# Layer 0 of a hybrid RWKV-7 / attention trunk: a pair's nine value products in one run behind its outputs, and the sample chunk's outputs as one full-array product

## The chip, the cores and the metric

The kernel runs on one core of a Trainium2 chip. A core has five engines with instruction queues of their own: TensorE (PE; its weight loads are listed as PEld), VectorE (DVE), ScalarE (ACT), GpSimd (POOL) and SyncE (SP), which issues the DMA transfers here. They meet through semaphores. The metric is the device time of one execution in microseconds (us); the time of a version is the median of its runs.

## The reference

The reference is one inference step of a two-layer encoder trunk on 512 prompt tokens and 32 sample tokens, with 1024 channels, in fp32. Layer 0 mixes tokens by an RWKV-7 recurrence, layer 1 by differential attention; both add a four-head memory attention, a SiLU gate, an output projection and a residual. What matters here is the recurrence of layer 0, which each of 24 heads with 64 channels runs over the tokens:

```python
def step(S, inp):
    r_t, k_t, v_t, w_t, kk_t, a_t = inp
    sa = jnp.einsum('bhvk,bhk->bhv', S, -kk_t)
    S = (S * w_t[:, :, None, :] + sa[..., None] * (kk_t * a_t)[:, :, None, :]
         + v_t[..., None] * k_t[:, :, None, :])
    return S, jnp.einsum('bhvk,bhk->bhv', S, r_t)
```

S is a 64x64 state. The prompt starts from a zero state, the sample from a given one. Each head returns its outputs y and the last state.

## The kernel before

**Chunks and pairs.** The recurrence is computed in chunks of 64 tokens: chunks 0 to 7 are the prompt, chunk 8 is the sample. Two heads together fill 128 partitions and are one of 12 pairs. Within a chunk the step becomes small matrices: `at` (`ats` for the sample) holds, per chunk, the decayed scores and the inverse of a triangular system; `sv` (`svs`) holds the values in one half of the partitions and, once solved, the corrections in the other half; `bt` (`bts`) holds decayed keys; `zr` decayed queries. The chain of a chunk (`chunk`, L806) has three parts, each after a `yield`:

- a: `zr` times the state, then a VectorE addition into `avz` (not for chunk 0);
- b: the inverse times `avz` (the solve), two ScalarE copies of the result into `sv`, and, except for chunk 0, the ScalarE copy `yt` of a's other half and the scaled state `sd`;
- c: `bt` times `sv`, from which VectorE forms the next state in `SB` (prompt) or `SS` (sample).

`ps_c` are the PSUM tiles of the chain (pool `psc`, two buffers). `avz` is one tile for all chunks and pairs; it must hold, before a chunk's solve, the product of the chunk's scores with its values. These are the value products of `rw_values` (L782): for each chunk and each head of the pair one product with 64 rows and 64 columns, a quarter of the 128x128 array. An even chunk uses rows 0 to 63 and output columns 64 to 127, an odd one the other two halves. ScalarE copies them from PSUM (`ps_v`, pool `psm`, two buffers) into `avz`. The outputs (`rw_outputs`, L865; `outputs`, L799) are products of 128 rows and 64 columns, half of the array, into `ps_yc` (pool `psx`, one buffer), which VectorE adds to `yt`.

A product in fp32 is two instructions with a weight load each in the trace; the main products below use operands split in advance into a high and a low part, one instruction each.

**The order of work.** While layer 0 runs, `ordered` is set, and each engine's instructions are tied into the order in which the program issues them (`Queue`, `tie`): every queue is strictly in that order. The program writes it by a plan. The projections of the layer ("main products", PSUM tiles `ps_g`, 128x272 outputs, 48 to a block of weights) are a generator from which single products are drawn. `PLAN` (L49) has 23 steps for a pair; each step issues the next part of the chain (step 0 is b of chunk 0, step 1 its c, steps 2, 3, 4 are a, b, c of chunk 1, and steps 20, 21, 22 are a, b, c of chunk 7), and then two halves with listed pieces: `(kind, pair offset, TensorE cost, VectorE cost)`. The pieces are `prep` (the preparation of a later pair, some thirty small parts), `inv`, `back`, `at`, `mrg` (the triangular inverse on GpSimd, its transfers, its merge on TensorE), `val` (values), `out` (outputs), `fin` (norm and gate), `smp` (the sample chunk). After the pieces of each half, `some` may issue one or two put-off functions (weight splits, evacuation work on ScalarE and VectorE), and then main products are drawn while the counted time t is below the half's due time:

```python
while left and t + MAIN / 2 < (due[k + 1] if half else (due[k] + due[k + 1]) / 2):
    next(main)
    t += MAIN
    left -= 1
```

t adds up the plan's costs, 0.27 for a chain part (`HOP`) and 0.126 for a main product (`MAIN`). The due times divide the sum of all of a pair's costs into 23 equal steps where a pair has 144 main products or more; most pairs have 192.

**Around the change.** Before, the values come in two pieces. Step 21 of the pair before does chunks 0 and 8 (`("val", 1, 0.45, 0)`), step 0 of the pair itself chunks 1 to 7 (`("val", 0, 0.95, 0)`). Step 22 has the pair's outputs, and in its second half the part of the third-next pair's `prep` that computes two exponentials on ScalarE (`de`, and `di` in the place of `cum`). Step 0 has a transpose of that prep (`ps_rt`). Pair 0's values are made in a lead-in of four pieces ahead of the loop, as far as the first value piece goes. From pair 9 on there is no third-next pair, and memory attention takes the place of the prep.

The sample chunk is run by `smp` pieces; its outputs are two half-array products into the fourth quarter of its own `ps_c` tile (`self.outputs(st, (c,), ps, 3)`), added to `yt` by one VectorE instruction.

## Time and profile before

| | |
|---|---|
| median of 3 runs | 1459.28 us (1458.47 to 1459.82) |
| span of the profiled execution | 1461.1 us, its only time on record, 1.8 us over the median |
| TensorE busy | 1403.8 us, 96% of the span |
| VectorE, ScalarE, GpSimd busy | 915.4, 831.6, 421.5 us |
| mean granted TensorE clock | 0.986 |
| a middle pair of layer 0 | 45.9 us (for example from 330.6 to 376.5) |
| `ps_v<-sv,at`, prompt values | 384 records on TensorE |
| `ps_v<-svs,ats`, sample values | 48 records |
| `ps_yc<-sv,at`, prompt outputs | 384 records |
| `ps_c<-svs,ats`, sample outputs | 48 records |
| `avz<-ps_v`, value copies on ScalarE | 36: 12 each of 64x256, 64x384 and 64x512 |

A row of a timeline gives the start, the busy time, the engine, the line, the operation, the tiles (out<-in), for TensorE the part of the array that is used (rows*columns), the shape and how many instructions were merged into it; in brackets, how long the engine stood idle before it and what released it. L103 is the helper through which nearly every instruction goes, so tiles tell them apart. Tile names leave out buffer numbers; `cum` is also the place of `di`. The busy time of a TensorE row is modelled and overlaps with the next; the distance from start to start is what a row costs. The chain runs on a small set of tile names: `ps_c<-avz,at` is b, `ps_c<-sv,bt` is c, `ps_c<-SB,zr` is a.

### The profile page before, as it was taken

The page shows a single profiled execution, that of the slowest core. Times are in us where ns is not written, and L with a number is a line of the kernel's source. Part 1 is how long each engine was busy: PE and PEld are TensorE (multiplying, and loading weights), DVE is VectorE, ACT ScalarE, POOL GpSimd, SP SyncE. Part 2 cuts the span into 40 slices and gives each one's busy share as a digit, 9 for nine tenths or more (in the row PEclk, how much of TensorE's full clock was granted, in tenths as well). Part 3 has the DMA queues.
Part 4 walks back from the last instruction along what each step waited for, and adds up shares of the span by engine and source line. Part 5 has one row for each costly group of instructions (what it writes and reads, how often), then busy time and mean ns, then how long its engine had stood idle before and what let it go on. Part 6 is the DMA issues. An engine that isn't in the chain of part 4 may idle for free.

```text
span 1461.1 us, 32131 instructions
## 1 busy us (share of the span) xinstructions
PE 1403.8 (96%) x11978; PEld 1320.5 (90%) x11978; DVE 915.4 (63%) x2313; ACT 831.6 (57%) x2269; POOL 421.5 (29%) x868
## 2 busy tenths in 40 slices
PE   6998899999999999899899999999999999999997
PEld 5997899999999998798799998999989999899997
DVE  7565777787877877565733565664466745657533
ACT  6664667667677676565533365653466546565322
POOL 2025576566766557500210040100001002100200
PEclk9998999999999999999999999999999999999999
DMA  6442122332223222232554473232323222322321
GB/s 217 128 129 71 32 71 76 81 81 70 79 74 81 73 77 63 70 98 76 185 158 121 126 198 102 78 87 84 113 67 89 84 87 81 88 83 75 102 87 69
DMA packets 266534, 139.20 MB, mean 95 GB/s; under 512 B 57658, under 2 KB 256579, under 8 KB 266379
## 3 DMA queue, kind: packets, MB, share of 16 engines
q1 hardware_dynamic: 266378, 137.16, 33.1%
q8 instruction: 94, 1.54, 0.4%
q14 instruction: 62, 0.50, 0.1%
HBM read 110.98 MB, written 22.78 MB: 92 GB/s over the span
## 4 chain that ended last, share of the span: by engine, by line
PE 81%; DVE 8%; ACT 4%; issue 2%; DMA 2%; POOL 2%; SPq 1%; DVEq 0%; ACTq 0%; POOLq 0%
PE ps_g L103 56%; PE ps_c L103 4%; PE ps_s L103 3%; PE ps_o L103 2%; PE ps_at L103 2%; DVE wlo L103 1%; PE ps_v L103 1%; PE ps_mm L103 1%; SPq L103 1%; PE ps_mo L103 1%; POOL tm L721 1%; PE ps_ss L103 1%; PE ps_aT L103 1%; DVE pt L103 1%; PE ps_yc L103 1%
## 5 line engine op out<-in xcount | busy, mean ns | idle before, releaser
L103 PE MATMUL ps_g<-hh,wlo 128*128 128x272 f32 x1808 | 541.3, 299 | 1.4 <-DVE wlo L103 1.4
L103 PE MATMUL ps_g<-hh,whi 128*128 128x272 f32 x1808 | 540.1, 299 | 0.1
L103 PE MATMUL ps_g<-hl,whi 128*128 128x272 f32 x1808 | 535.6, 296 | 0.0
L103 DVE TENSOR_TENSOR wlo<-raw,whi 128x512 fp32r<-128x512 f32 x322 | 230.9, 728 | 205.6 <-ACT whi L103 196.2
L103 PEld LDWEIGHTS ps_g<-hh,wlo 128*128 128x128 f32 x1808 | 343.6, 190 | 6.4 <-DVE wlo L103 2.1
L103 PEld LDWEIGHTS ps_g<-hh,whi 128*128 128x128 f32 x1808 | 344.1, 190 | 4.4 <-PE ps_g L103 0.3
L103 PEld LDWEIGHTS ps_g<-hl,whi 128*128 128x128 f32 x1808 | 343.7, 190 | 3.6
L103 ACT CAST whi<-raw 128x512 fp32r<-128x512 f32 x322 | 194.7, 617 | 186.1 <-PE ps_g L103 132.6
L721 POOL TENSOR_TENSOR tm<-u,m 102x84 f32<-102x84 f32 (+23 forms) x372 | 158.3, 426 | 183.5 <-DMA m<-sc 155.4
L723 POOL TENSOR_TENSOR u<-u,tm 102x84 f32<-102x84 f32 (+23 forms) x372 | 158.5, 426 | 29.1
L103 PE MATMUL ps_g<-hi,whi 128*128 128x272 f32 x512 | 149.8, 292 | 0.9 <-ACT hi L103 0.9
L103 PE MATMUL ps_g<-lo,whi 128*128 128x272 f32 x512 | 148.4, 290 | 1.8 <-DVE lo L103 1.3
L103 PE MATMUL ps_g<-hi,wlo 128*128 128x272 f32 x512 | 148.3, 290 | 0.8 <-DVE wlo L103 0.8
L1706 POOL TENSOR_TENSOR kz<-k,kh 64x544 fp32r<-64x544 f32 x24 | 34.7, 1446 | 325.0 <-ACT kh L103 324.1
L103 PEld LDWEIGHTS ps_g<-lo,whi 128*128 128x128 f32 x512 | 96.9, 189 | 2.7 <-DVE lo L103 1.8
L103 PEld LDWEIGHTS ps_g<-hi,whi 128*128 128x128 f32 x512 | 97.0, 190 | 1.6 <-ACT hi L103 1.1
L103 PEld LDWEIGHTS ps_g<-hi,wlo 128*128 128x128 f32 x512 | 96.9, 189 | 1.1 <-DVE wlo L103 1.1
L103 DVE SCALAR_TENSOR_TENSOR SB<-ps_c,dl,sd 64x64 f32<-64x64 f32 x168 | 47.4, 282 | 49.0 <-PE ps_c L103 43.4
L103 ACT ACTIVATE pt<-ps_s,snm 128x128 f32<-128x128 f32 (+3 forms) x96 | 50.8, 530 | 23.8 <-DVE snm L103 23.0
L103 ACT COPY sv<-ps_c 64x64 f32<-64x64 f32 x192 | 39.5, 206 | 39.5 <-PE ps_c L103 37.7
L103 ACT ACTIVATE sg<-ps_g 128x272 f32<-128x272 f32 x64 | 25.3, 396 | 48.0 <-PE ps_g L103 45.5
L1161 POOL TENSOR_TENSOR lo<-og,hi 128x544 fp32r<-128x544 f32 x8 | 13.7, 1713 | 131.0 <-issue 130.5
(364 smaller groups left out, 2614.1 us busy)
## 6 DMA issues: line engine op xcount, KB each, us to landing
raw<-in_rw_in_dram SPq DMA_DIRECT2D x114, 256.0 KB
raw<-in_df_in_dram SPq DMA_DIRECT2D x112, 256.0 KB
raw<-in_w_out_dram SPq DMA_DIRECT2D x64, 256.0 KB
m<-sc SPq DMA_DIRECT2D x36, 128.0 KB
oscr<-sg SPq DMA_DIRECT2D x16, 272.0 KB
lo<-oscr SPq DMA_DIRECT2D x16, 272.0 KB
raw<-in_w_mem_k_dram SPq DMA_DIRECT2D x16, 256.0 KB
raw<-in_w_mem_v_dram SPq DMA_DIRECT2D x16, 256.0 KB
```

Of the source, the lines that this page charges most:

```text
L103: return lambda *a, **k: self.trunk.tie(self, issue(*a, **k))
L721: nc.gpsimd.tensor_tensor(tm[:, :n, :wd], u3[:, :n, kx : kx + 1].to_broadcast(sh), m3[:, kx : kx + 1, kx + 1 :].to_broadcast(sh), ALU.mult)
L723: nc.gpsimd.tensor_tensor(u3[:, :n, kx + 1 :], u3[:, :n, kx + 1 :], tm[:, :n, :wd], ALU.add)
L1161: (self.nc.gpsimd if g % 2 else self.ve).tensor_tensor(lo[:], t, hi[:].bitcast(F32), ALU.subtract)
L1706: nc.gpsimd.tensor_tensor(kz[rows[m], m, :], k[rows[m], :], hi.bitcast(F32), ALU.subtract)
```

## The change

The values of a pair become one piece, at step 22 of the pair before, behind the outputs and ahead of the exponentials: nine chunks, 18 products in one run, odd and even chunks in turn (1 with 0, 3 with 8, 5 with 2, 7 with 4, then 6 alone), into three PSUM tiles, one of them from the chain's pool `psc` and two from `psm`. Three ScalarE copies follow: chunks 0 and 8, then 2, 4, 6, then 1, 3, 5, 7. In the plan the pieces at step 0 (0.95) and step 21 (0.45) go, and one of cost 1.0 comes. In the lead-in all nine chunks of pair 0 are made where the first piece was.

The sample chunk's outputs become one product of the full array, 128 rows, 128 columns; only its two diagonal blocks are used. They lie in different partitions, so VectorE adds them to `yt` by two instructions in place of one.

```diff
-    [[("val", 0, 0.95, 0), ("prep", 2, 0.1, 0)], [("prep", 2, 0, 0.42)]],
+    [[("prep", 2, 0.1, 0)], [("prep", 2, 0, 0.42)]],
...
-    [[("prep", 3, 0, 1.45), ("val", 1, 0.45, 0)], [("prep", 3, 0, 0.5)]],
-    [[("out", 0, 1.6, 0.7)], [("prep", 3, 0, 0)]]]
+    [[("prep", 3, 0, 1.45)], [("prep", 3, 0, 0.5)]],
+    [[("out", 0, 1.6, 0.7), ("val", 1, 1.0, 0)], [("prep", 3, 0, 0)]]]
...
-        for sets in (((0, 8),), ((1, 3, 5, 7), (2, 4, 6))):
-            yield
-            ps = [self.psm.tile([P, 4, P], F32, tag="m", name=f"ps_v{cs[0]}") for cs in sets]
-            for j in range(len(sets[0])):
-                for h in range(2):
-                    for q, cs in zip(ps, sets):
-                        if j < len(cs):
-                            _, zs, ro, A, cv, _ = self.place(st, cs[j])
-                            self.te.matmul(q[zs, j, H[h]], A[0][ro, h, :], cv[ro, H[h]], start=True, stop=True)
-            for q, cs in zip(ps, sets):
-                e, zs = self.place(st, cs[0])[:2]
-                i = slice(0, 5, 4) if cs[0] == 0 else slice(cs[0] // 2, 4)
-                self.ae.copy(avz[zs, e, i, :], q[zs, : len(cs)])
+        yield
+        ps = [pool.tile([P, 4, P], F32, tag=tag, name=f"ps_v{i}")
+              for i, (pool, tag) in enumerate(((self.psc, "c"), (self.psm, "m"), (self.psm, "m")))]
+        sets = ((0, 8), (2, 4, 6), (1, 3, 5, 7))
+        for odd, even in zip((1, 3, 5, 7, None), (0, 8, 2, 4, 6)):
+            for h in range(2):
+                for c in (odd, even):
+                    if c is not None:
+                        q, cs = next((q, cs) for q, cs in zip(ps, sets) if c in cs)
+                        _, zs, ro, A, cv, _ = self.place(st, c)
+                        self.te.matmul(q[zs, cs.index(c), H[h]], A[0][ro, h, :], cv[ro, H[h]], start=True, stop=True)
+        for q, cs in zip(ps, sets):
+            e, zs = self.place(st, cs[0])[:2]
+            i = slice(0, 5, 4) if cs[0] == 0 else slice(cs[0] // 2, 4)
+            self.ae.copy(avz[zs, e, i, :], q[zs, : len(cs)])
...
         if c == 8:
-            self.outputs(st, (c,), ps, 3)
+            self.te.matmul(ps[:, 3, :], A[1].rearrange("p h t -> p (h t)"), cv, start=True, stop=True)
...
         if c == 8:
-            self.ve.tensor_tensor(yt[:64, 4, :], ps[:64, 3, :], yt[:64, 4, :], ALU.add)
+            for hc in H:
+                self.ve.tensor_tensor(yt[:64, 4, hc], ps[hc, 3, hc], yt[:64, 4, hc], ALU.add)
```

## The prediction

> **What bounds the kernel now.** I read the page first, then TensorE's waits, then the timelines of TensorE and ScalarE around one change of pairs, since the change works only there and at the sample chunk.
>
> ```profile
> span 1461.1 us, 32131 instructions
> PE 1403.8 (96%) x11978; PEld 1320.5 (90%) x11978; DVE 915.4 (63%) x2313; ACT 831.6 (57%) x2269; POOL 421.5 (29%) x868
> ```
>
> TensorE is busy 96% of the span. ScalarE's 57% looks harmless, but it is a mean over the program. The stretch from 281 to 289 us, where pair 2 ends and pair 3 begins, says something else:
>
> ```profile
> 281.00:289.00 8.00, 8.00 (x108) 7.44 (x108) 3.90 (x11) 7.30 (x21) 6.75 (x17) 1.00 0.37 107
> ```
>
> The columns after the length are the busy us of TensorE, its weight loads, VectorE, ScalarE and GpSimd, then the granted clock. TensorE is full, at full clock, and ScalarE has 0.70 us free in 8. What moves TensorE's work here must be asked of ScalarE too. TensorE's starts there:
>
> ```profile
> 281.10 0.38 PE L103 MATMUL ps_c<-avz,at 128*128 128x128 f32 x2
> 281.42 0.44 PE L103 MATMUL ps_v<-sv,at 64*64 64x64 f32 x4
> 281.70 0.39 PE L103 MATMUL ps_v<-svs,ats 64*64 64x64 f32 x4
> 282.02 0.39 PE L103 MATMUL ps_g<-hh,whi 128*128 128x272 f32 x1
> 282.25 0.29 PE L103 MATMUL ps_g<-hl,whi 128*128 128x272 f32 x1
> ...
> 283.12 0.38 PE L103 MATMUL ps_c<-sv,bt 128*128 128x128 f32 x2
> 283.44 1.15 PE L103 MATMUL ps_yc<-sv,at 128*64 128x64 f32 x32
> 284.52 0.40 PE L103 MATMUL ps_g<-hh,wlo 128*128 128x272 f32 x1
> 284.75 0.39 PE L103 MATMUL ps_c<-avz,at 128*128 128x128 f32 x2
> 285.07 1.14 PE L103 MATMUL ps_v<-sv,at 64*64 64x64 f32 x28
> 286.14 0.33 PE L103 MATMUL ps_rt<-ident,rr 128*128 128x128 f32 x1
> 286.22 0.37 PE L103 MATMUL ps_g<-hh,whi 128*128 128x272 f32 x1
> ...
> 286.92 0.38 PE L103 MATMUL ps_c<-sv,bt 128*128 128x128 f32 x2
> ...
> 288.90 0.38 PE L103 MATMUL ps_c<-SB,zr 128*128 128x128 f32 x2
> ```
>
> The ps_c rows are the chain: chunk 7's solve (281.10) and state product (283.12), chunk 0's solve (284.75) and state product (286.92), chunk 1's first product (288.90). I call them b7, c7, b0, c0, a1; b7 to a1 takes 7.80 us with 28 main products (ps_g) between: 8, 1, 5 and 14. A count is of records; one product of full precision is two. ScalarE, in its program order:
>
> ```profile
> 281.51 0.47 ACT L103 ACTIVATE ta<-ps_wa,dv 128x272 f32<-128x272 f32 x1
> 281.89 0.41 ACT L103 COPY sv<-ps_c 64x64 f32<-64x64 f32 x2
> 282.31 0.26 ACT L103 COPY yt<-ps_c 64x128 f32<-64x128 f32 x1
> 282.59 0.40 ACT L103 ACTIVATE sd<-SB,dl 128x128 f32<-128x128 f32 x1
> 283.02 0.37 ACT L103 COPY avz<-ps_v 64x256 f32<-64x256 f32 x1
> 283.41 0.67 ACT L103 ACTIVATE de<-cum 128x553 f32<-128x553 f32 x1
> 284.11 0.67 ACT L103 ACTIVATE cum<-cum 128x553 f32<-128x553 f32 x1
> 284.95 0.39 ACT L103 COPY raw<-ps_g 128x272 f32<-128x272 f32 x1 [0.17 <-PE ps_g L103]
> 285.23 0.30 ACT L103 COPY yt<-avz 64x128 f32<-64x128 f32 x1
> 285.54 0.42 ACT L103 COPY sv<-ps_c 64x64 f32<-64x64 f32 x2
> 286.24 1.08 ACT L103 COPY avz<-ps_v 64x512 f32<-64x512 f32 x2 [0.28 <-PE ps_v L103]
> ```
>
> Two orders matter. The two big value copies (1.08) come behind chunk 0's sv copies (end 285.96); and the exponentials of the prep (de, cum) run at 283.41, before chunk 0's solve. What a state product waits for is shown one pair earlier:
>
> ```profile
> 189.36 0.26 ACT L103 COPY yt<-ps_c 64x128 f32<-64x128 f32 x1
> ```
>
> ```profile
> 189.67 0.30 PEld L103 LDWEIGHTS ps_c<-sv,bt 128*128 128x128 f32 x2 [0.18 <-ACT yt L103]
> 190.09 1.01 PEld L103 LDWEIGHTS ps_yc<-sv,at 128*64 128x64 f32 x32
> ```
>
> ```profile
> 193.89 0.30 PEld L103 LDWEIGHTS ps_c<-sv,bt 128*128 128x128 f32 x2 [0.49 <-ACT sv L103]
> ```
>
> It starts 0.05 us after the end of the yt copy (189.62). Chunk 0 has no such copy; its state product was last released by sv (193.89). A c product that has waited takes 0.42 to the next start (189.67 to 190.09), one that has not 0.32 (283.12 to 283.44). Seven main products from 282.25 to 283.12 make 0.124 each; c0 to a1, 1.98, less 14 of these leaves 0.24 for two full records, 0.12 each.
>
> **The change, part by part.** *The plan.* Taking 0.95 from step 0 and 0.45 from step 21 and adding 1.0 to step 22 lowers a middle pair's sum by 0.40, so a step falls from 1.964 to 1.947 plan-us. Step 0 now counts 0.37 instead of 1.32 ahead of its main products: 13 in place of 5. Step 1 gets 13 for 14. Step 22 counts 0.27 + 1.6 + 1.0 = 2.87, more than a step, so it gets none for 1, and step 21 gets 4 for 8. b7 to a1 now holds 4 + 0 + 13 + 13 = 30.
>
> *b7 to c7.* Eight value records (281.42 to 282.02) and four main products leave. TensorE would be ready at 281.10 + 0.24 + 4 x 0.124 = 281.84. But c7 waits for the yt copy, whose work and predecessors are unchanged: 282.57 + 0.05 = 282.62. So 1.52 us for 2.02: -0.50, with 0.78 us of new idle. What is late is ScalarE's queue: ta, sv, sv, yt.
>
> *c7 to b0.* c7 takes 0.42, now that it waits; the outputs with their exit 1.08 (283.44 to 284.52). Of the 28-record run (1.07), the exit and four records in one quarter are known from the short visit (281.42, 281.70, 282.02: four records 0.28, four with the exit 0.32, so some 0.06 a record and 0.14 the exit); that leaves 0.03 for each of the 24 alternating ones, and eight more make 1.31. The switch from half to quarter arrays is not in the trace: free would be 0.12 less; I take the exit price, as a change of mode, and keep 0.12 below for the range. Sum 2.81 for 1.63: +1.18. In this segment one main product (0.23) leaves.
>
> *b0 to c0.* This decides. In program order ScalarE now has the three value copies, then the exponentials, then yt and sv of chunk 0. The copy of chunks 0 and 8 is early: chunk 8 stands in the second of four groups, so it runs beside the rest of the run and b0 does not wait. The others need the run's end; today the first starts 0.10 after it (286.14 to 286.24). From b0: 0.10 + 1.08 copies + 0.03 + 1.37 exponentials (283.41 to 284.78) + 0.02 + 0.30 yt + 0.01 + 0.42 sv + 0.05 = 3.38 us. TensorE meanwhile has b0 0.24, ps_rt 0.08 (286.14 to 286.22) and 13 x 0.124 = 1.61: 1.93 us. It idles 1.45; segment 3.38 for 2.17: +1.21. Nothing fills the hole, since c0 stands at the head of TensorE's queue and all main products of step 1 behind it. The raw, shc and rkv work of the finished block moves ahead of the value copies, into ScalarE's wait for them: free, or 0.39 more if the block's evacuation (284.95) were late.
>
> *c0 to a1.* One main product less, 0.10 for the restart: -0.02.
>
> The sum is -0.50 + 1.18 + 1.21 - 0.02 = +1.87; two main products more than before, 0.25, are missing elsewhere in the pair: **+1.62 us** per change of pairs. The same with no waits at all: b7 to c7 0.74, then 2.71, 1.93 and 1.86, less 0.25, is 6.99 for 7.80: -0.81. That is what the new order saves in array time.
>
> *Which boundaries.* There are eleven. In the first nine the prep of a third pair puts its exponentials there: 9 x 1.62 = 14.6. In the last two there are none; without their 1.37 the wait at c0 vanishes, but both ps_m buffers are held by value copies when the next products want them. I take +0.6 each (between -0.81 and +1.62): 1.2. Pair 0's own values move into the lead-in; TensorE's waits name the merge's transposes later in pair 0, and that wait covers the move either way.
>
> *Sample chunk.*
>
> ```profile
> 305.01 0.39 PE L103 MATMUL ps_c<-svs,bts 128*128 128x128 f32 x2
> 305.32 0.45 PE L103 MATMUL ps_c<-svs,ats 128*64 128x64 f32 x4
> 305.70 0.39 PE L103 MATMUL ps_g<-hh,wlo 128*128 128x272 f32 x1
> 305.93 0.29 PE L103 MATMUL ps_g<-hh,whi 128*128 128x272 f32 x1
> ```
>
> ```profile
> 305.96 0.58 DVE L103 SCALAR_TENSOR_TENSOR SS<-ps_c,dl,sd 64x64 f32<-64x64 f32 x2
> ```
>
> Four half-array records with their entry and exit become two full ones: 305.01 + 4 x 0.12 + 0.124 puts the second ps_g at 305.61 in place of 305.93, -0.32 (-0.2 if the entry were not the price that it looks). VectorE gets one more 64x64 addition; by half of a pair of them (305.96) about 0.29. It delays the sums queued behind it; the next chunk's solve hides that, and if its cover were gone it would cost 0.3. Eleven pairs count, as pair 0's gain goes into the wait above: -3.5.
>
> Total: 14.6 + 1.2 - 3.5 = +12.3 us. The profiled span of 1461.1 becomes 1473.4; the page gives no longer time of that execution, and the span stands 1.8 above the median of the runs, so I predict 1459.3 + 12.3 = **1471.6**.
>
> [...]
>
> **The rivals.** *The array time decides (faster).* If c7 and c0 find their operands ready, each boundary gains 0.81 and the sample chunk 0.32: 11 x 1.13 = 12.4, so 1446.9. For it: the entries and exits around 281.42, 283.44 and 285.07, of which one pair is left. Against it: ScalarE's 7.30 of 8. It decides if ScalarE has chunk 0's sv within 1.93 us of b0 instead of 3.38, as it would with the exponentials ahead of the value copies, and yt before 281.84.
>
> *Only c0 waits.* If c7's wait is covered (ScalarE reaches sv and yt earlier), 0.78 at each of eleven boundaries goes: 12.3 - 8.6 = +3.7, 1463.0. The 0.47 us of ta in front of sv speaks against it.
>
> *The edits cancel.* If only c7 waits, nine times 1.45 goes: 12.3 - 13.0 = -0.7, 1458.6, no change. It needs main products between b0 and c0 that the plan does not have, or shorter exponentials.
>
> *The waits spread.* If the held ps_m buffers and the late copies also hold up the next pair's prep, by 0.6 a boundary: +6.6, 1478.2.
>
> **How the numbers follow.** My sum 0.69, only c0 waits 0.09, array time 0.13, cancel 0.04, spread 0.05. The sum's own range is 1467 to 1476: down 1.3 for a free switch and 2.8 for the last two boundaries at -0.81, up 1.3 for the smaller sample gain and 2.0 for the last two at +1.62, and about 1 for the first boundary, whose work around it differs. A measurement of this kernel tells about 0.2%, 2.9 us, from no change. So faster 0.13, same 0.05, slower 0.82. The range 1462 to 1478 holds the main case, the one wait and part of the spread, about 0.8.
>
> **What would show it.** Right: c0 after each of nine boundaries starts 0.05 after ScalarE's sv, with an idle of about 1.4 before it; ScalarE's order there is three avz, de, cum, yt, sv; c7 waits about 0.8 for yt; ps_v and ps_yc stand in one unbroken run; the sample rows show x2 full products. Wrong: no idle before c0, or the exponentials ahead of the avz copies; then the array time wins and the forecast is off by over 20 us. If the c7 wait alone is missing, I misjudged what stands ahead of yt.

## The result, and the profile after

The changed kernel takes 1476.8 us (median of four executions; 1473.95 to 1495.83), the kernel before, run beside it, 1459.6. The ratio on record is 1.0148, 95% interval 1.0116 to 1.0180. It goes by all executions, and the one of 1495.83 lifts it; the medians alone make 1.0118. The forecast was 1471.6. The direction was right; of the loss of 17 us between the medians the forecast had 12. By the ratio the loss is some 22 us, which makes about 1481, and that lies above the range of the prediction.

The two counts at the head of the page of the changed kernel's profiled execution:

```profile
span 1472.2 us, 32129 instructions
PE 1392.4 (95%) x11954; PEld 1311.6 (89%) x11954; DVE 919.8 (62%) x2325; ACT 831.8 (56%) x2269; POOL 411.4 (28%) x868
```

TensorE is busy 11.4 us less than before, in a span that is 11.1 us longer: about 22 us of idle came in. Up to 6 of the 11.4 us can be the clock, since this execution was at half clock for 30.6 us and that of before for 42.7; the rest is saved array time. The same change of pairs as in the prediction, one pair later, by windows (length; busy us of TensorE, weight loads, VectorE, ScalarE, GpSimd; granted clock):

```profile
333.40:341.40 8.00, 6.49 (x98) 5.80 (x98) 3.24 (x12) 7.11 (x20) 6.66 (x18) 1.00 0.46 128
```

TensorE was busy all 8 us before; now it is busy 6.49, and ScalarE still 7.11. TensorE's starts there (timeline):

```profile
332.74 0.39 PE L103 MATMUL ps_c<-avz,at 128*128 128x128 f32 x2
...
334.25 0.49 PE L103 MATMUL ps_c<-sv,bt 128*128 128x128 f32 x2 [0.63 <-ACT yt L103]
334.67 1.15 PE L103 MATMUL ps_yc<-sv,at 128*64 128x64 f32 x32
335.75 0.50 PE L103 MATMUL ps_v<-sv,at 64*64 64x64 f32 x9
...
336.27 0.87 PE L103 MATMUL ps_v<-sv,at 64*64 64x64 f32 x20
337.07 0.49 PE L103 MATMUL ps_c<-avz,at 128*128 128x128 f32 x2
337.39 0.27 PE L103 MATMUL ps_rt<-ident,rr 128*128 128x128 f32 x1
...
340.18 0.49 PE L103 MATMUL ps_c<-sv,bt 128*128 128x128 f32 x2 [0.88 <-ACT sv L103]
...
342.14 0.27 PE L103 MATMUL ps_c<-SB,zr 128*128 128x128 f32 x1
```

Both waits of the forecast are there: c7 on yt (334.25) and c0 on sv (340.18). b7 to a1 is 332.74 to 342.14, 9.40 us for 7.80. ScalarE's queue shows why c0 is late:

```profile
336.48 0.37 ACT L103 COPY avz<-ps_v 64x256 f32<-64x256 f32 x1 [0.34 <-PE ps_v L103]
337.17 1.07 ACT L103 COPY avz<-ps_v 64x384 f32<-64x384 f32 x2 [0.32 <-PE ps_v L103]
338.14 0.67 ACT L103 ACTIVATE de<-cum 128x553 f32<-128x553 f32 x1
338.84 0.67 ACT L103 ACTIVATE cum<-cum 128x553 f32<-128x553 f32 x1
339.41 0.28 ACT L103 COPY yt<-avz 64x128 f32<-64x128 f32 x1
339.70 0.42 ACT L103 COPY sv<-ps_c 64x64 f32<-64x64 f32 x2
```

Three value copies, two exponentials, yt, sv; c0 starts 0.06 us after sv ends. TensorE's waits over the whole span, the changed kernel's largest few (us in total, times, longest):

```profile
PE ps_w L103 <- DVE t1b L103: 11.1, 22, 2.8
PE ps_c L103 <- ACT yt L103: 9.9, 14, 2.0
PE ps_c L103 <- ACT sv L103: 8.3, 9, 1.3
...
PE ps_at L103 <- DVE bk L103: 4.9, 10, 1.5
```

Nine waits on sv, one for each of nine changes of pairs, as forecast. But the first row and the last have nothing to do with the values: 22 waits for `t1b`, the transposes with which the merge of a later pair begins, and ten for `bk`, one of the key products of a later pair. The kernel before has six and two of them:

```profile
PE ps_w L103 <- DVE t1b L103: 7.3, 6, 3.7
...
PE ps_at L103 <- DVE bk L103: 1.0, 2, 0.7
```

These waits the prediction does not have. VectorE's rows at step 17, after and then before:

```profile
371.29 0.79 DVE L103 SCALAR_TENSOR_TENSOR rkv<-raw,PA,rkv 128x544 f32<-128x544 f32 x1
372.12 0.90 DVE L103 STREAM_TRANSPOSE t1b<-at 32x256 f32<-32x256 f32 x2
```

```profile
364.53 0.90 DVE L103 STREAM_TRANSPOSE t1b<-at 32x256 f32<-32x256 f32 x2
365.37 0.73 DVE L103 SCALAR_TENSOR_TENSOR rkv<-raw,PA,rkv 128x544 f32<-128x544 f32 x1
```

The put-off addition `rkv` of a finished projection block has moved from behind the transposes to ahead of them. Nobody moved it: other main products per step let the blocks end elsewhere, and `some` issues their put-off work wherever it then stands. TensorE feels it at once:

```profile
372.61 0.24 PE L103 MATMUL ps_w<-t1b,at 32*32 32x32 f32 x2 [0.61 <-DVE t1b L103]
```

At step 7 the same addition (350.55 in the full trace) stands ahead of the second `bk` product, and TensorE waits for that.

### The profile page after: what moved, and what is told of

Same layout as the page of the kernel before. It is cut to its first block, busy times and chain, and to the rows that moved or that the text cites. A ratio compares the mean times of both kernels' runs of the same rounds, so it can differ in the third digit from the quotient of the medians.

```text
span 1472.2 us, 32129 instructions
## 1 busy us (share of the span) xinstructions
PE 1392.4 (95%) x11954; PEld 1311.6 (89%) x11954; DVE 919.8 (62%) x2325; ACT 831.8 (56%) x2269; POOL 411.4 (28%) x868
## 4 chain that ended last, share of the span: by engine, by line
PE 79%; DVE 8%; ACT 6%; DMA 3%; issue 2%; SPq 1%; POOL 0%; DVEq 0%; POOLq 0%; ACTq 0%
PE ps_g L103 54%; PE ps_c L103 4%; PE ps_s L103 3%; PE ps_o L103 2%; PE ps_at L103 2%; PE ps_v L103 1%; SPq L103 1%; PE ps_mm L103 1%; PE ps_mo L103 1%; DVE rkv L103 1%; PE ps_w L103 1%; ACT sv L103 1%; PE ps_yc L103 1%; PE ps_aT L103 1%; DVE wlo L103 1%
## 5 line engine op out<-in xcount | busy, mean ns | idle before, releaser
L721 POOL TENSOR_TENSOR tm<-u,m 102x84 f32<-102x84 f32 (+23 forms) x372 | 154.5, 415 | 209.2 <-DMA m<-sc 181.1
L723 POOL TENSOR_TENSOR u<-u,tm 102x84 f32<-102x84 f32 (+23 forms) x372 | 153.7, 413 | 29.0
L103 DVE SCALAR_TENSOR_TENSOR SB<-ps_c,dl,sd 64x64 f32<-64x64 f32 x168 | 47.5, 283 | 46.4 <-PE ps_c L103 39.6
L103 PE MATMUL ps_c<-sv,bt 128*128 128x128 f32 x192 | 40.4, 292 | 18.5 <-ACT yt L103 9.9
L103 PEld LDWEIGHTS ps_c<-sv,bt 128*128 128x128 f32 x192 | 30.0, 191 | 24.1 <-ACT yt L103 13.6
```

What stands on the lines that cost most here:

```text
L103: return lambda *a, **k: self.trunk.tie(self, issue(*a, **k))
L721: nc.gpsimd.tensor_tensor(tm[:, :n, :wd], u3[:, :n, kx : kx + 1].to_broadcast(sh), m3[:, kx : kx + 1, kx + 1 :].to_broadcast(sh), ALU.mult)
L723: nc.gpsimd.tensor_tensor(u3[:, :n, kx + 1 :], u3[:, :n, kx + 1 :], tm[:, :n, :wd], ALU.add)
```

## The experiments

All times are medians. The ratios are those on record, to the kernel before on the same chip; they go by all executions and are not quotients of the medians. A "clean pair" is one of pairs 1 to 8 in which the profiled execution shows no half clock, from its b0 to the next. The column "half clock" is how long TensorE ran at half clock within these eight pairs, in the profiled execution. The last column is span times mean granted clock, the mean over all executions of a kernel: what the span would be at full clock if TensorE set the pace throughout. It is an estimate, good to about 1 us, and tells a change in the work from a change in the clock.

| kernel | us | ratio (95%) | clean pair, us (median) | half clock, us | span x clock, us |
|---|---|---|---|---|---|
| before | 1459.6 to 1461.2 | 1 | 45.9 | 6.8 | 1441.3 to 1441.6 |
| after | 1476.8 | 1.0148 (1.0116 to 1.0180) | 47.8 | 3.4 | 1456.9 |
| sample_only | 1459.5 | 0.9992 (0.9979 to 1.0006) | 45.9 | 3.4 | 1439.6 |
| values_only | 1483.1 | 1.0140 (1.0115 to 1.0164) | 48.0 | 3.7 | 1459.5 |
| old_costs | 1482.8 | 1.0141 (1.0122 to 1.0159) | 47.6 | 6.8 | 1455.3 |
| run_at_21 | 1461.6 | 1.0009 (0.9996 to 1.0022) | 45.8 | 6.8 | 1440.7 |
| run21_even | 1483.2 | 1.0148 (1.0128 to 1.0167) | 47.4 | 20.5 | 1450.8 |
| exps_first | 1481.8 | 1.0148 (1.0114 to 1.0182) | 47.4 | 23.9 | 1453.0 |
| merge_first | 1472.6 | 1.0074 (1.0056 to 1.0092) | 47.6 | 7.9 | 1453.5 |
| copies_split | 1473.9 | 1.0089 (1.0071 to 1.0108) | none | 27.8 | 1445.4 |
| filled | 1467.1 | 1.0056 (1.0042 to 1.0070) | 46.6 | 0 | 1448.7 |
| queue_order | 1466.9 | 1.0059 (1.0035 to 1.0082) | 46.9 | 10.3 | 1447.3 |
| queue_split | 1458.4 | 0.9992 (0.9977 to 1.0008) | 45.6 | 10.2 | 1436.5 |
| queue_moved | 1456.4 | 0.9980 (0.9969 to 0.9990) | 45.6 | 0.5 | 1438.2 |
| after_moved | 1475.4 | 1.0108 (1.0095 to 1.0121) | 47.6 | 0 | 1455.6 |
| before_moved | 1462.0 | 1.0015 (1.0006 to 1.0023) | 46.5 | 0 | 1445.4 |

### The two edits apart

sample_only is the kernel before with the last two hunks of the diff alone (one full product, two additions). values_only is the changed kernel without them.

> Only the sample chunk's full-array product and its two additions; values and plan as before. By the forecast's step each pair saves 0.32 us of TensorE between the sample's state product and the next main product, and eleven pairs show it: -3.5 us, ratio about 0.9976. Rival: the second VectorE addition holds up the next chunk's addition and the gain is lost: 0 us. A third outcome, slower, would mean that the sample edit has part in the loss.

> Only the values' run behind the outputs, with its plan; the sample chunk as before. If the two edits simply add, it is slower than the changed kernel by the sample's 3.5 us, so some +15 to +20 us against before. If the sample edit does harm together with the run, it is faster than the changed kernel.

The sample step itself shortens from 2.02 to 1.67 us, the forecast's 0.32 and a little. In the kernel before almost none of it arrives: two steps later the pair is 0.15 longer, and 0.1 goes at steps 19 and 20, so a clean pair is 45.9 us in both and the time does not change measurably. In the changed kernel it is worth 0.2 to 0.4 in a clean pair (values_only against after), but the two kernels' ratios do not tell them apart. values_only lost 22 us between the medians, where 15 to 20 were expected. The whole loss is the values'.

### The plan's counts, and the place of the run

old_costs keeps the changed kernel's order but gives the plan the counts of before. The piece at step 22 is counted as nothing, and two further pieces carry the old 0.95 and 0.45 and issue nothing, since the run is already made.

```diff
-    [[("prep", 2, 0.1, 0)], [("prep", 2, 0, 0.42)]],
+    [[("val", 0, 0.95, 0), ("prep", 2, 0.1, 0)], [("prep", 2, 0, 0.42)]],
...
-    [[("prep", 3, 0, 1.45)], [("prep", 3, 0, 0.5)]],
-    [[("out", 0, 1.6, 0.7), ("val", 1, 1.0, 0)], [("prep", 3, 0, 0)]]]
+    [[("prep", 3, 0, 1.45), ("val", 0, 0.45, 0)], [("prep", 3, 0, 0.5)]],
+    [[("out", 0, 1.6, 0.7), ("val", 1, 0, 0)], [("prep", 3, 0, 0)]]]
```

> The changed kernel, but the plan counts 0.95 at step 0 and 0.45 at step 21 as before (by a piece with nothing left to do) and 0 at step 22, so that every main product and every put-off function stands in the step where it stood before. Theory: the waits inside a pair, away from its ends (steps 7 and 17, 0.42 and 0.82 us longer in the changed kernel), come from put-off VectorE additions that the new plan moved ahead of the merge's transposes and the key products; they go. The wait at chunk 7's state product falls from 0.63 to about 0.3, as eight main products stand ahead of it; the idle before chunk 0's state product grows from 0.9 to about 2, as only five do. In all chunk 7's solve to chunk 1's first product about 9.6 us for 7.8 with the same 28 main products: +1.8 a boundary, sample -0.3, so about +14 us. Rival: the waits of steps 7 and 17 follow from the late start of the pair itself (everything on ScalarE late by the boundary's loss); then they stay, and it is +24 us or more.

Steps 7 and 17 are back at 2.01 and 2.08 us: the two VectorE waits come from the counts. But with the five main products of before between b0 and c0 in place of 13, the hole there is larger (TensorE's timeline):

```profile
341.60 0.49 PE L103 MATMUL ps_c<-sv,bt 128*128 128x128 f32 x2 [2.04 <-ACT sv L103]
```

b7 to a1 is 1.52 + 3.04 + 3.16 + 2.08 = 9.80, +2.00. The forecast's +1.87 is for 30 main products, and these are the 28 of before, so the two do not compare as they stand; b0 to c0, which by the forecast ScalarE alone decides, is 3.16 for its 3.38.

The time misses what was expected: 1482.8 is 22 us above before, for 14. It is not the rival, since both waits are gone. By span times clock the kernel is 14 us above before (1455.3 against 1441.3), as expected, so the other 8 us are the clock: its executions have mean clocks of 0.981 to 0.985 where those of before on the same chip have 0.985 to 0.991.

run_at_21 moves the run one step up, between b7 and c7, with the old counts; run21_even is the same program order with the old counts exchanged between the two steps.

```diff
-    [[("prep", 3, 0, 1.45)], [("prep", 3, 0, 0.5)]],
-    [[("out", 0, 1.6, 0.7), ("val", 1, 1.0, 0)], [("prep", 3, 0, 0)]]]
+    [[("prep", 3, 0, 1.45), ("val", 1, 0.45, 0)], [("prep", 3, 0, 0.5)]],
+    [[("out", 0, 1.6, 0.7)], [("prep", 3, 0, 0)]]]
```

(run_at_21 has 0.95 for `val` at step 0 as in old_costs; run21_even has 0.45 at step 0 and 0.95 at step 21.)

> All nine values in one run, but at step 21, between chunk 7's solve and its state product, with the plan's counts of before (so no main product and no put-off function moves); sample chunk as changed. Theory (the order of ScalarE's queue is what costs): the run covers the wait for chunk 7's copies, the value copies fall beside outputs and main products, and the exponentials end early: chunk 7's solve to chunk 1's first product about 7.7 us for 7.8 before and 9.4 changed, chunk 0's state product waits at most 0.5. With the sample's gain -0.4 us a pair, about -5 us: ratio 0.996. Rival (the run of nine costs by itself, by its switch of array shape or its three PSUM tiles, wherever it stands): it stays slower than before by 5 us or more.

> The run of the nine chunks' value products one step earlier than in the changed kernel, between the solve and the state product of chunk 7, and the plan's counts as before the change spread (0.95 and 0.45 main blocks' worth on the steps where the kernel before had them), the sample chunk as changed. The run at that place with other counts gave 1461.6 us with 2.87 us for its own step and no wait behind it. If only position and ScalarE's order cost, this is the same to within 2 us: 1459 to 1463, middle pairs of 45.6 to 46.0 us, no wait on bk or t1b above 0.2 us. If the count of main products in front of each step matters as much as the position, the pairs shift by 0.3 us or more, 3 us in all, either way.

With the run one step earlier there is no wait at c0 or c7, and b7 to a1 is 2.87 + 1.62 + 1.42 + 1.98 = 7.89. The time is that of before; the gain of 5 us that was expected did not come, and neither did the rival's loss. So the merged run is not dear in itself. One wait is new (run_at_21, TensorE's timeline):

```profile
375.75 0.33 PE L103 MATMUL ps_rt<-ident,rr 128*128 128x128 f32 x1 [0.25 <-DVE yt L103]
```

`ps_rt` and the outputs' `ps_yc` share the one buffer of `psx`, and VectorE adds the outputs to `yt` just then: from b0 to `ps_rt` it is 0.63 us, for the 0.24 of two full records. And the last 20 records of the run take 0.042 us each there, against 0.034 in the changed kernel; why is open. So this run does not show what the saved array time is worth. copies_split, below, gives an estimate: its b7 to a1 of 8.24 us, less the one wait in it (c7 on yt, 0.63) and its two main products more (0.25), is 7.36, which is 0.44 below 7.80, about half of the 0.81 that the prediction's first rival counts on. run21_even missed by 20 us: the exchange of 0.5 us between two counts brought the waits for t1b and bk back (step 17 2.9, step 7 2.35) and, in four of eight pairs, the half clock. That is as much as the whole change cost. By span times clock half of it is work (1450.8 against 1440.7) and half is the clock (0.980 against 0.986 in the mean of the executions).

### ScalarE's order

exps_first (the first diff below) issues the exponentials' part of the prep ahead of the values; copies_split (the second) gives the copies of the even and the odd set to VectorE.

```diff
-    [[("out", 0, 1.6, 0.7), ("val", 1, 1.0, 0)], [("prep", 3, 0, 0)]]]
+    [[("out", 0, 1.6, 0.7), ("prep", 3, 0, 0), ("val", 1, 1.0, 0)], []]]
```

```diff
-            self.ae.copy(avz[zs, e, i, :], q[zs, : len(cs)])
+            (self.ae.copy if cs[0] == 0 else self.ve.tensor_copy)(avz[zs, e, i, :], q[zs, : len(cs)])
```

> The changed kernel with one entry of the plan moved: in the last step of a pair the two exponentials of the next pair (de, cum; 0.67 us each) are issued ahead of the value products and their three copies, so that ScalarE does de, cum, avz x3, yt, sv in place of avz x3, de, cum, yt, sv. Theory 1 (ScalarE's order between the value copies and sv holds the first state product of a pair): the wait before that state product (0.88 us, ps_c<-sv,bt on ACT sv) goes to at most 0.3, and part of it comes back as a later first copy, since the copies now stand behind 1.34 us of exponentials while the products take 0.80: step c7 to b0 grows from 2.81 by up to 0.5, step b0 to c0 falls from 3.11 to 2.2 to 2.5. Net -0.2 to -0.6 us for a pair, -2 to -6 us in all: 1471 to 1475 where the changed kernel has 1476.8. Theory 2 (the run of products itself is what costs, ScalarE's order is only where it shows): the two steps together stay at 5.9 us and the time at 1476 to 1478. Steps 7 and 17 (2.4 and 2.9 us) stay as they are by both.

> The changed kernel with two of the three copies of the values out of PSUM given to VectorE (the sets of four and of three; the set with chunk 0 stays on ScalarE). Theory 1 (ScalarE's order holds the first state product): ScalarE is free for the exponentials some 0.7 us sooner, sv comes 0.7 us sooner, step b0 to c0 falls from 3.11 to 2.3 to 2.5 us; -5 to -7 us in all, 1470 to 1472, if VectorE has the 1.2 us to spare at that place; if it has not, what VectorE does next (the transposes of the merge, the additions of the masks) is late by as much, and steps 18 to 22 or 0 to 3 grow by 0.3 to 0.6 us: 1473 to 1477. Theory 2 (the run itself costs): no change at b0 to c0, 1476 to 1478.

In both, b0 to c0 falls from 3.11 to 2.06, what TensorE needs there: ScalarE's order was the cause of that wait. With the exponentials ahead, b0 pays for it (timeline of exps_first, TensorE and then ScalarE):

```profile
382.97 0.49 PE L103 MATMUL ps_c<-avz,at 128*128 128x128 f32 x2 [0.71 <-ACT avz L103]
```

```profile
381.17 0.66 ACT L103 ACTIVATE de<-cum 128x553 f32<-128x553 f32 x1
381.86 0.67 ACT L103 ACTIVATE cum<-cum 128x553 f32<-128x553 f32 x1
382.55 1.34 ACT L103 COPY avz<-ps_v 64x256 f32<-64x256 f32 x3
```

c7 to b0 grows from 2.81 to 3.59, and a clean pair gains 0.35. With the copies on VectorE nothing comes back at this place: b7 to a1 is 8.24, 1.16 less than after. And yet exps_first takes 1481.8 us, with the changed kernel's ratio of 1.0148, where 1471 to 1475 were expected. copies_split takes 1473.9; between the medians that is 3 us less than the changed kernel, or 4.5 if each is taken against before on its own chip, where nine times 1.16 is 10. By span times clock the two gain 4 and 11.5 us on the changed kernel, so the work did shorten and the clock took it back (0.981 and 0.982 in the mean of the executions, 0.985 in the changed kernel). Both have long steps 17 and 18 in pair after pair (exps_first from pair 5 on), 3.4 to 4.0 and 2.4 to 3.4 us, in which the main products start 0.23 us apart where 0.125 is usual. The clock is the next experiment.

### The half clock

The granted clock of copies_split, by windows, in pair 4, with the same stretch of the pair in the kernel filled below (the columns as above; the clock is the number after GpSimd's):

```profile
366.50:369.90 3.40, 2.59 (x46) 2.25 (x46) 2.68 (x7) 1.24 (x4) 2.77 (x9) 1.00 0.48 135
369.90:373.30 3.40, 3.40 (x16) 3.40 (x17) 3.16 (x11) 3.05 (x9) 2.85 (x8) 0.51 0.06 15
```

```profile
362.70:366.10 3.40, 3.06 (x51) 2.70 (x50) 2.69 (x7) 1.24 (x3) 2.77 (x9) 1.00 0.23 64
366.10:369.50 3.40, 3.40 (x27) 3.38 (x28) 3.16 (x11) 3.14 (x10) 2.93 (x7) 1.00 0.06 16
```

All stretches at half clock last 3.41 us or a multiple (but for the one that the program's end cuts off), and in one execution all begin at whole multiples of 3.41 us from each other: in before the trace's clock records have 3.413, 6.827 and 10.240 us, and the starts lie 32, 44, 72, 153, 171 and 204 times 3.413 us behind the first. A window below is one of these steps of 3.41 us. In the middle pairs nearly all begin 34 to 37 us after b0, so the window before holds the end of step 16 and the start of step 17: ten products of 2 columns (`ps_ss`, the norm's sums) that take 1.1 us, and 32 of 32 columns (`ps_w`, the merge) that take 0.6 to 0.9. I counted, over the traces of all kernels of the table, the columns that TensorE streamed in each full-clock window from 192 to 555 us (a main product is 272; by the measured 0.124 to 0.125 us each I estimate some 7400 columns for a window of nothing else). All 29 windows that were followed by a half-clock one streamed 1700 to 3474. Of the 1641 others 24 had under 3300, and none under 2436. So each half clock there came behind a window with few columns, but not each such window was followed by one. If each product's columns count by the share of the array's 128 rows that it uses, the 29 windows have at most 2706, and only 10 of the 1641 others have so few. Outside the middle pairs even that does not tell them apart: the changed kernel's window from 617.6 us on has 1920 columns, 1472 by this share, and was not followed by a half-clock one.

TensorE was at work in the windows ahead: in copies_split it was busy 2.59 of the 3.40 us of the first row above, and no wait there was longer than 0.62 us; in before and queue_split none was longer than 0.07.

The test adds dead work. filled is copies_split with four products of 256 columns, whose result nobody reads, where TensorE waits for t1b:

```diff
         ps = self.psx.tile([P, 512], F32, tag="x", name="ps_w1")
+        for _ in range(4):
+            self.te.matmul(ps[:, 256:], self.hh[:, 0, :P], self.hh[:, 0, :256], start=True, stop=True)
```

> The kernel with two value copies on VectorE, and in front of the merge's first products (step 17, where TensorE waits 0.4 to 0.6 us for t1b) four more products of 256 columns whose result is not used: 1024 columns, 0.45 us. Theory (the clock is halved for a window of 3.41 us after a window in which few columns were streamed; at steps 16 and 17 the merge's small products and the wait leave 1700 to 3200 columns in a window): with 1024 more the half-clock windows at step 17 go in nearly all pairs, the pairs fall from 47.7 to 46.7 us or a little over, and the time from 1473.9 to 1463 to 1467, though work was added. Rival (the halving does not follow from what TensorE does there): the windows stay in six or more of the nine pairs and the time is 1473 to 1478.

The half clock at step 17 is gone from all eight pairs, the pairs are 46.4 to 46.8, and the kernel is faster for doing more: by 6.9 us between the medians, by 5 if each is taken against the kernel before on its own chip (1.0089 and 1.0056). The whole stretch of the middle pairs, in copies_split and then in filled:

```profile
237.00:560.00 323.00, 311.83 (x3113) 297.78 (x3109) 257.70 (x626) 219.91 (x629) 194.25 (x432) 0.97 0.29 74
```

```profile
237.00:560.00 323.00, 313.75 (x3210) 298.36 (x3207) 263.48 (x647) 224.26 (x642) 207.82 (x443) 1.00 0.29 74
```

The clock also accounts for the spread of the changed kernel. Its four executions have spans of 1472.2, 1473.7, 1494.1 and 1476.4 us with mean clocks of 0.990, 0.989, 0.974 and 0.987; span times clock is 1457.5, 1457.5, 1455.3 and 1457.2. A pair of 47.8 us is 14 windows of the 3.413 us in the clock records, so step 17 can stand at nearly the same place in a window pair after pair. In copies_split it does: seven of its half-clock stretches, from 274.4 to 561.1 us, begin 47.8 us apart. That the same happened in the execution of 1494.1 is not shown, as only the one of 1472.2 has a trace.

### VectorE's order

merge_first (the first diff below) issues the merge's transposes ahead of the put-off work of step 16. queue_order (the second) closes three half-steps (the first halves of 6, 16 and 17) for put-off work, with the mark that the plan has for it, and moves nothing else.

```diff
-    [[("prep", 3, 1.04, 0.17)], [("mrg", 1, 0, 0.86)]],
+    [[("prep", 3, 1.04, 0.17), ("mrg", 1, 0, 0.86)], []],
```

```diff
-    [[("prep", 2, 0, 1.1), ("smp", 0, 0.21, 0.29)], [("prep", 2, 0, 0.86)]],
+    [[("prep", 2, 0, 1.1), ("smp", 0, 0.21, 0.29), FULL], [("prep", 2, 0, 0.86)]],
...
-    [[("prep", 3, 1.04, 0.17)], [("mrg", 1, 0, 0.86)]],
-    [[("mrg", 1, 0.9, 0)], [("rsq", 0, 0, 1.5)]],
+    [[("prep", 3, 1.04, 0.17), FULL], [("mrg", 1, 0, 0.86)]],
+    [[("mrg", 1, 0.9, 0), FULL], [("rsq", 0, 0, 1.5)]],
```

> The changed kernel with one entry of the plan moved: the merge (its cast and four transposed copies start here, with t1b) is issued ahead of the put-off blocks of step 16, not after them. Theory 1 (a put-off VectorE addition of 0.79 us in front of t1b makes TensorE wait at step 17): step 17 falls from 2.90 to 2.1 us, the waits of ps_w on t1b of 0.4 us and more go, and the pair shortens by 0.7 to 0.85 us, 6 to 8 us in all: 1469 to 1471 where the changed kernel has 1476.8; step 7 stays at 2.4. Theory 2 (GpSimd's inverses set the pace of a pair, and the wait at step 17 only shows there): the next step that needs the inverse takes the wait over, step 17 shortens and steps 18 to 20 grow by as much, and the time stays within 2 us of 1476.8.

> The changed kernel with three half-steps of the plan (first halves of steps 6, 16 and 17) closed for put-off work, so that VectorE's additions and weight splits stand behind the transposes and the square roots as they did before the change; nothing else is moved. Theory (the part that the prediction missed is VectorE's order: 0.42 us at step 7, 0.82 at step 17 of a pair): step 7 falls from 2.43 to 2.0, step 17 from 2.90 to 2.1, step 19 does not grow to 2.7 as it did with the merge alone moved; a middle pair without a half-clock window is 46.2 to 46.6 us where the changed kernel has 47.65; in all -8 to -11 us, 1466 to 1469. Rival (GpSimd or some other pace of 47.6 us holds the pair): other steps grow by as much and the pairs stay at 47.4 or more.

With the merge alone moved, step 17 falls to 2.10 and step 19 grows from 2.05 to 2.73, for VectorE (merge_first, TensorE's timeline):

```profile
374.39 0.41 PE L103 MATMUL ps_y<-ident,yt 128*128 128x128 f32 x2 [0.69 <-DVE yt L103]
```

A weight split still stands ahead of the square roots on which `yt` depends. So the clean pair is hardly shorter, as its second theory said, though the wait moved along VectorE's queue, not GpSimd's. Its 4 us, which are in neither theory's range, come from the first pairs; pair 0 is 45.9 us for 48.6 after, with 5.0 us at half clock in place of 10.4. With all three places closed, steps 7 and 17 are 2.15 and 2.10, step 19 is 2.0 to 2.3, and the clean pair is 46.7 to 46.9: 0.9 less than after, short of the 46.2 to 46.6 that were expected. The time is 9.8 us less between the medians, as expected, and 9.6 by span times clock.

### Both repairs, and main products between the low stretches

queue_split is queue_order with copies_split. queue_moved, after_moved and before_moved take queue_split, the changed kernel and the kernel before, and lower one count, so that six main products more are drawn in step 16, between `ps_ss` and `ps_w`, and as many fewer elsewhere:

```diff
-    [[("prep", 3, 1.04, 0.17)
+    [[("prep", 3, 0.3, 0.17)
```

> Both repairs: put-off work closed at the three half-steps, and two of the three value copies on VectorE. If the terms add (1.24 us of VectorE's order, 0.95 of ScalarE's order in a pair), a middle pair is 45.4 to 45.7 us, shorter than the 45.93 before the change: 1453 to 1457. If the half-clock windows take it back (they stand at step 17 of nearly every pair with the copies split alone), the pairs with such a window are 1.0 to 1.5 us longer; with the wait at step 17 gone there should be fewer of them, 2 to 4 in the nine pairs: then 1456 to 1461. If VectorE has no room for the copies once its order is changed: waits on yt or bk of 0.3 us or more in each pair, 1460 to 1466.

> Put-off work closed at the three half-steps, two value copies on VectorE, and the plan's TensorE cost of step 16's prep lowered from 1.04 to 0.3, so that six main products more stand between the norm's sums (10 products of 2 columns, 1.1 us) and the merge's first products (32 of 32 columns, 0.9 us), and as many fewer elsewhere. Theory (a window of 3.41 us with less than some 3200 streamed columns is followed by one at half clock): the two low stretches no longer fall into one window, no half-clock window stands at step 17, all middle pairs are 45.4 to 45.8 us, and the time is 1452 to 1456 where the same without the move had 1458.4 and the kernel before 1459.6. Rival (the six products are missed where they are taken away, or the clock is halved elsewhere instead): pairs of 45.9 us or more, 1458 to 1462.

> The changed kernel with the same move of six main products into step 16. They also cover the wait for t1b at step 17, which the addition in front of it makes: six times 0.124 stand in TensorE's queue ahead of it. So step 16 grows by 0.75, step 17 falls from 2.90 to 2.1 to 2.3, and 0.5 us are saved elsewhere: pairs of 46.9 to 47.2 us for 47.65, no half-clock window at step 17: 1468 to 1472, with less spread than the 1474 to 1496 of the changed kernel. If the wait for yt takes the place of that for t1b (as with the merge moved alone), 1471 to 1475.

> Control: the kernel before with the same move. Its pairs 2 and 8 had a half-clock window at steps 17 and 18 each, 1.1 to 1.2 us longer; these go. Its other pairs, at 45.93, have no wait to cover and stay at 45.9 to 46.0. So 1456 to 1458, 0.1 to 0.25% below the kernel before; if the put-off addition now stands ahead of the square roots and yt comes late, step 19 grows and the time is 1460 to 1464.

The terms add: clean pairs of queue_split are 45.6 us, 0.3 below the kernel before. But in every second pair, from the one that begins at 284.0 on, step 17 is halved (queue_split, TensorE's timeline; the clock is halved from 410.9 on):

```profile
407.55 1.28 PE L103 MATMUL ps_ss<-hsel,sq 128*128 128x2 f32 x10
...
409.39 0.38 PE L103 MATMUL ps_c<-SB,zr 128*128 128x128 f32 x2
409.70 1.00 PE L103 MATMUL ps_w<-t1b,at 32*32 32x32 f32 x32
...
411.25 0.43 PE L103 MATMUL ps_g<-hh,whi 128*128 128x272 f32 x1
411.48 0.43 PE L103 MATMUL ps_g<-hl,whi 128*128 128x272 f32 x1
411.70 0.43 PE L103 MATMUL ps_g<-hh,wlo 128*128 128x272 f32 x1
```

With the products moved between them (queue_moved):

```profile
404.18 1.28 PE L103 MATMUL ps_ss<-hsel,sq 128*128 128x2 f32 x10
...
407.09 0.69 PE L103 MATMUL ps_w<-t1b,at 32*32 32x32 f32 x32
...
408.07 0.29 PE L103 MATMUL ps_g<-hl,whi 128*128 128x272 f32 x1
408.19 0.29 PE L103 MATMUL ps_g<-hh,wlo 128*128 128x272 f32 x1
```

no pair is halved at step 17, in any of the three kernels. queue_moved is the one version that is measurably faster than the kernel before, 0.9980 (0.9969 to 0.9990) of it, though 1456.4 is just above the 1452 to 1456 that were expected, and from queue_split it is not told apart. Its pairs 2 and 3 are 45.0 and 45.2 us; in pair 4 and each one after it TensorE waits 0.3 to 0.7 us for GpSimd, and these are 45.6 to 46.0 (TensorE's waits from 237 to 560 us):

```profile
PE ps_q L103 <- POOL rkk L647: 2.1, 5, 0.7
```

The control says that the move alone is no gain: before_moved is 0.15% slower, since step 19 now waits 0.4 for yt, the miss that its expectation names. after_moved has no half clock at step 17 either and is at 1475.4 (1475.0 to 1475.7, the spread gone) where 1468 to 1472 were expected; its clean pairs are 47.6, not 46.9 to 47.2, since six products fewer elsewhere let c0 wait 1.0 and bk 0.4. Between these two, where the half clock does not enter the pairs, the change costs 13.4 us.

## Why the prediction was right or wrong

The prediction's terms against the traces (pair 4 of the changed kernel and of the kernel before):

| step of the prediction | change forecast, us | change measured, us |
|---|---|---|
| b7 to c7 (2.02 before) | -0.50 | -0.51 |
| c7 to b0 (1.63 before) | +1.18 | +1.18 |
| b0 to c0 (2.19 before) | +1.21 | +0.92 |
| c0 to a1 (1.98 before) | -0.02 | -0.02 |
| two main products missing elsewhere | -0.25 | -0.25 |
| sample step | -0.32 | -0.35 |
| waits at step 7 and step 17 | no term | +0.30, +0.85 |
| other steps | no term | -0.4 |
| pair | +1.30 | +1.75 |

**Right.** Which waits come at the change of pairs, on what, and how often (nine on sv). c7's price to 0.01 us. c7 to b0: the switch from half to quarter arrays, which the trace of before did not show, costs what the prediction called the exit price: 0.15 from the last `ps_yc` to the first `ps_v`. The sample step at its own place. The first rival is excluded as the prediction put it: it asked for ScalarE to have sv within 1.93 us of b0, and it took 3.05.

**Too large: b0 to c0.** The working chained ScalarE's rows end to end. In the trace `de` starts 0.10 before the last value copy ends (337.17 + 1.07 against 338.14) and yt 0.10 before `cum` ends; the segment is 3.11 us, not 3.38. TensorE's own work in it is 2.06, not 1.93 (copies_split, where it does not wait), so it stands idle for 1.05 and not 1.45; the row's 0.88 counts from the modelled end of the last product.

**Wrong: "two main products more than before, 0.25, are missing elsewhere in the pair", as the plan's only effect outside the boundary.** The plan's new counts also put the block ends, and with them the put-off functions, in other steps. The prediction looked at this for ScalarE at the boundary alone ("free, or 0.39 more"), and not along VectorE's queue. That is +1.15 at steps 7 and 17 (step 7 grew by 0.42, of which 0.12 is one main product more), less some 0.4 in steps 2, 3 and 20, whose single causes were not followed up. With the 0.27 of c0 taken off, the pair is 0.45 above the forecast, about 4 us in nine, which is most of the 5 us that the forecast falls short. old_costs (both waits gone with the old counts) and queue_order (9.8 us back) show it.

**Not in the prediction at all: the clock.** It read one stretch at full clock and had no term for half-clock windows. By span times clock the change costs 15 to 16 us (1456.9 against 1440.6 to 1441.6), 3 to 4 more than forecast, as nine times the pair's 0.45 says too. What goes beyond that, in the execution of 1495.83 and in the ratio, is the clock.

**The rivals.** "The waits spread" is the nearest, in its time (1478.2) and in its idea, but not in its mechanism: VectorE's order held up the next pairs, not held ps_m buffers. That "the next chunk's solve hides" the second sample addition was right in the changed kernel and half wrong in the one before: in sample_only 0.15 of the 0.35 come back two steps later.

**The last two boundaries.** b7 to a1 grew by 1.05 and 0.78 us, where +0.6 each was taken. `ps_v` and `ps_mo` wait there for ScalarE's avz copies, 0.6 each: the held ps_m buffers. The first boundary, for which about 1 us was left open, grew by 2.39, where most of the others grew by 1.58.

**The profiled execution.** The predicted span was 1473.4 and the profiled one is 1472.2; that they agree is chance. It had 30.6 us at half clock where that of before had 42.7. Span times mean clock gives 1457.5 for it and 1440.6 for that of before: 17 us of work, as the medians say.

**The copies on ScalarE.** With two of the three value copies on VectorE (copies_split), b7 to a1 is 1.16 us shorter than in the changed kernel. In the time it brought 3 to 4.5 us by itself, of some 11 by span times clock, until VectorE's order and the half clock were mended too. What the first rival counts on was not measured: no version with the values in one run is free of every wait at that place, and the estimate from copies_split, 0.44, is about half of that rival's 0.81.

**What stays open.** Why the run's last records are slower between b7 and c7 (0.042 us for 0.034); what sets the windows that were followed by a half-clock one apart from the 24 with under 3300 columns that were not; what the saved array time is worth where nothing waits; and the small gains in the other steps.

## What to carry to other kernels

In a program whose order is drawn from counted costs, an edit's price is not only where it stands: list, for before and after, which put-off functions stand ahead of what on each engine's queue over the whole period, as the same code at the same place came out at 1461.6 and 1483.2 us by half a microsecond of counts, half of that through the clock. Read an engine's share in the stretch and its rows in program order, and let back-to-back instructions overlap a little where the trace shows it (0.10 us on ScalarE here). Look at the granted clock in every stretch before a wait is taken away: in copies_split the half clock at a stretch with few streamed columns left 3 to 4.5 us of a gain of 11.5, and four products of dead work put there (filled) were worth 5 to 7.

## What the hardware showed that was not expected

- TensorE's clock was halved for 3.41 us or a multiple although TensorE was at work in the window ahead: in the middle pairs no wait there was longer than 0.07 us in before, queue_order and queue_split, and none longer than 0.63 in the others, but for one of 2.8 in old_costs. These 29 windows had 1700 to 3474 streamed columns, where by my estimate main products back to back make some 7400. Four products of dead work (1024 columns) took 5 to 7 us off the time (filled against copies_split).
- The same kernel took 1474 to 1496 us, with mean clocks of 0.990 to 0.974; span times mean clock differed by 2.2 us.
- From the last half-array product to the first quarter-array one it is 0.15 us in the changed kernel's trace (at each of eleven places), as much as from the last quarter-array product to the first full one.
- On ScalarE an instruction can start before the one ahead of it ends, in the changed kernel's trace by 0.10 us in the median of 1049 such places and by 0.15 at most.
